# Hybrid decoder block: x loaded by token, plain float32 first products, and turns moved around the rotations and the second norm

## The chip, the cores and the metric

One core of a Trainium2 chip runs the kernel. The metric is the device time of one execution in microseconds (us); three runs are given by their median. The engines are TensorE (PE; its weight loads are PEld), VectorE (DVE), ScalarE (ACT), GpSimd (POOL) and SyncE (SP), whose queue issues nearly all loads.

## The reference

x has 256 tokens of 2048 features, c is one conditioning vector, all float32.

```python
mod = silu(c) @ w_ada + b_ada                       # 2048 -> 6 x 2048
shift1, scale1, gate1, shift2, scale2, gate2 = split(mod, 6)
h = rms_norm(x, norm1_g) * (1 + scale1) + shift1
qa, ka, va, qr, kr, vr, gr, ga_logit, gb_logit = split(h @ w_in, ...)
qa, ka = rms_norm per head                          # 8 heads of 128
ya = softmax(qa ka^T * 128**-0.5 + bias[distance], causal) va @ w_attn_br
qr, kr = rotary(qr), rotary(kr) * 128**-0.5         # 8 heads of 128
yr = (group_norm((qr kr^T * decay) vr) * silu(gr)) @ w_ret_br
x = x + gate1 * ((sigmoid(ga_logit) * ya + sigmoid(gb_logit) * yr) @ w_o)
h2 = rms_norm(x, norm2_g) * (1 + scale2) + shift2
val, gt = split(causal_conv3(h2 @ w_up) + conv_b, 2)     # 2 x 5632
out = x + gate2 * ((silu(gt) * val) @ w_down)
```

## The kernel before, in words

**Products.** A float32 product is made of three products of the type float32r: each operand is split into hi (an ACT cast) and lo (a DVE subtraction, `split`, line 133), and hi hi, lo hi and hi lo are added up in PSUM. Activations are the stationary side (128 features x 128 tokens), weights the moving side (512 columns). Weights come in tiles of 128 x 1024 (512 KB, tag raw, nine buffers, shared with w_ada); such a chunk is 12 products of 512 columns for the two halves of the tokens (t = 0, 1). `row_block` (214) runs one 256 x 512 result through its chunks, with two PSUM banks of eight.

**First norm (231 to 271).** x comes transposed (xT, features on partitions). Squares are summed over the tiles on ACT and DVE, a product with a matrix of ones sums over the partitions, and rstd is 128 x 256. `modulated` (262) loads four halves of w_ada for each 128 features; each half is one DVE product with silu(c), summed into `parts` (`ada`, 170). `norm_tile` (250) then makes scale and shift with single-column operations and multiplies x by rstd (both on POOL from k = 2 on), applies scale and shift on ACT, and splits: h1[k].

**First products (274 to 300).** Six groups of 1024 columns (q, k, rotary q, k, and gr) need h1[0] to h1[10] in the steps k = 0 to 2, 3 to 5 and 6 to 10; in a step each group runs its k's and is added into `acc`. The other five k's follow in `finish_block` (314; 2.5 chunks a block of 512 columns).

**What sets the order.** The code is written once, straight through, and a planner orders each engine's instructions ahead of time by program order, readiness and its own estimate of durations; on the chip every engine then works in that order. `keep_in_program_order` pins an instruction among the pinned ones. The class `Side` (50) mixes in side work: after each chunk `pump` counts down every active generator (`yield 6` sleeps six chunks) and runs those that are due, a little ahead in priority; at most `width` are active, others wait in a queue. A paced generator issues w_ada halves at a rate a chunk (0.75, later 0.46 and 0.38), and `until` forces it.

**Rotations.** After each of the blocks 4 to 7 (499) a generator `rotated(n)` is put at the front of the side queue. It gives POOL, for each t, two multiplications by sin (487), one by cos (489) and one addition (490), sleeps six chunks, and turns the result with 16 transposes (r_t, 339). Blocks 8 to 11 follow (gr, with silu). The attention heads (three active at a time; scores, softmax with scalings on POOL at 452, turn, product with va) share that queue. Retention (514) sleeps three chunks before its turn (rpt, 549).

**Second norm (637 to 663).** Four w_o blocks, each added to x2 with gate1 (642, 643) and squared with a sum on ACT (644); then rstd2 for all tokens, a scaling on DVE (654), transposes (xt, 587), scale and shift on ACT (661) and the split into h2; then 22 blocks of w_up and 8 of w_down.

Of the kernel before, what the change touches and what calls it, by code (L numbers as in the profile page):

```python
# [11 lines left out]
F32 = mybir.dt.float32  # L12
# [17 lines left out]
K2 = STEPS[-1][1]  # L30
ADA_FIRST = 0.75
ADA_RATE = 0.46
ADA_LAST = 0.38
SIDE_AHEAD = 150
FH = FT // 2
# [56 lines left out]
def block_kernel(ctx, tc, a, out):  # L92
# [19 lines left out]
    def bank(name):  # L112
        return psum.tile([P, 512], F32, tag="ps", name=name)
# [6 lines left out]
    xT = cpool.tile([P, KC, S], F32, tag="x", name="xT")  # L120
    for q in range(4):
        nc.sync.dma_start(xT[:, 4 * q:4 * q + 4, :], a["xT"][:, 4 * q:4 * q + 4, :])
    ones = cpool.tile([P, P], F32, name="ones")
    nc.vector.memset(ones, 1.0)
# [5 lines left out]
    mod = cpool.tile([P, NADA], F32, name="mod")  # L130

# [30 lines left out]
    def load_split(src, w, name):  # L162
        raw = wpool.tile([P, 1024], F32, tag="raw", name=f"raw_{name}", bufs=9)
        nc.sync.dma_start(raw[:, :w], src)
        hi = wpool.tile([P, 1024], F32R, tag="hi", name=f"hi_{name}")
# [4 lines left out]
    def ada(jt, pin=False):  # L170

        for h in range(2):
            t = wpool.tile([P, 1024], F32, tag="raw", name=f"ada_{jt}_{h}", bufs=9)
            nc.sync.dma_start(t, a["w_ada"][jt, h])
            ins = nc.vector.scalar_tensor_tensor(t, t, 1.0, crow[:, h * 1024:(h + 1) * 1024],  # L175
                                                 op0=ALU.mult, op1=ALU.mult, accum_out=parts[:, jt, h:h + 1])
            if pin:

                tc.keep_in_program_order(ins)
            yield  # L180
# [7 lines left out]
    def scales_of(eng, j0, n, g_col):  # L188

        m = mod[:, j0:j0 + n]  # L190
        eng.tensor_scalar_add(m, m, 1.0)
        eng.tensor_tensor(m, m, sm[:, g_col:g_col + n], op=ALU.mult)

    def tok(act, part, t):

        return act[part][:, t * P:(t + 1) * P]
# [17 lines left out]
    def row_block(dram, acts, name):  # L214

        ps = [bank(f"{name}_{t}") for t in range(2)]
        n = len(acts)
        for k0 in range(0, n, 2):
# [4 lines left out]
        return ps  # L223

# [6 lines left out]
    sums = []  # L231
    for q in range(8):
        sq = tmp(f"sq1_{q}", (P, 2, S))
        xq = xT[:, 2 * q:2 * q + 2, :]
        if q == 7:
            nc.vector.tensor_tensor(sq, xq, xq, op=ALU.mult)
        else:
            nc.scalar.activation(sq, xq, AF.Square)
        if q > 1:
            nc.vector.tensor_tensor(sq, sq, sums.pop(0), op=ALU.add)  # L240
        sums.append(sq)
    nc.vector.tensor_tensor(sums[1], sums[0], sums[1], op=ALU.add)
    nc.scalar.activation(warm, crow[:, D - 1:], AF.Sqrt, bias=eps, scale=0.0)
    stat = bank("stat1")
    for k in range(2):
        nc.tensor.matmul(stat[:, :S], ones, sums[1][:, k, :], start=(k == 0), stop=(k == 1))
    rstd = cpool.tile([P, S], F32, name="rstd")
    h1 = []

    def norm_tile(k):  # L250
        eng = nc.vector if k < 2 else nc.gpsimd
        mods_of(eng, KC + k, 1)
        mods_of(eng, k, 1)
        scales_of(eng, KC + k, 1, C_G1 + k)
        t = tmp(f"ht_{k}")
        eng.tensor_tensor(t, xT[:, k, :], rstd, op=ALU.mult)
        nc.scalar.activation(t, t, AF.Identity, bias=mod[:, k:k + 1], scale=mod[:, KC + k:KC + k + 1])
        h = unit(f"h1_{k}", F32R)
        split(h[:, 0], h[:, 1], t)
        return h[:, 0], h[:, 1]  # L260

    def modulated():
        for k in range(KC):
            yield from ada(KC + k, pin=(k == 0))
            yield from ada(k, pin=(k == 0))
            h1.append(norm_tile(k))

# [3 lines left out]
    rstd_of(rstd, stat[:, :S], 1.0 / D)  # L271


    acc = [[None, None] for _ in range(2 * NG)]
    for step, (ka, kb) in enumerate(STEPS):
        for g in range(NG):
            banks = [[bank(f"g{step}_{g}_{j}_{t}") for t in range(2)] for j in range(2)]
            for k in range(ka, kb):
                side.until(lambda: len(h1) > k)
                hi, lo = load_split(a["w_g"][k, g], 1024, f"g_{g}_{k}")  # L280
                for part, w in ((0, hi), (1, hi), (0, lo)):
                    for t in range(2):
                        for j in range(2):
                            nc.tensor.matmul(banks[j][t], tok(h1[k], part, t), w[:, j * NB:(j + 1) * NB],  # L284
                                             start=(k == ka and part == 0 and w is hi),
                                             stop=(k == kb - 1 and w is lo))
                side.pump()
            for j in range(2):
                for t in range(2):
                    n = 2 * g + j  # L290
                    if step == 0:
                        acc[n][t] = unit(f"acc_{n}_{t}", shape=(P, NB))
                        nc.scalar.copy(acc[n][t], banks[j][t])
                    elif j == 0:
                        e = tmp(f"ev{step}_{n}_{t}", (P, NB))
                        nc.scalar.copy(e, banks[j][t])
                        nc.gpsimd.tensor_tensor(acc[n][t], acc[n][t], e, op=ALU.add)
                    else:
                        nc.vector.tensor_tensor(acc[n][t], banks[j][t], acc[n][t], op=ALU.add)
# [4 lines left out]
    def rest_of_mod():  # L304
        for jt in range(2 * KC, 6 * KC):
            yield from ada(jt, pin=True)
            if jt % KC == KC - 1:
                j0 = jt + 1 - KC
                mods_of(nc.gpsimd, j0, KC)
                if j0 == 4 * KC:  # L310
                    scales_of(nc.gpsimd, j0, KC, C_G2)
            mods[0] = jt + 1
# [8 lines left out]
    x2 = cpool.tile([P, 2, D], F32, tag="x", name="x2")  # L321
    cosT = cpool.tile([P, 2, P // 2], F32, name="cosT")
    sinT = cpool.tile([P, 2, P], F32, name="sinT")
    for dst, src in ((sm[:, C_CW:], a["small"][:, C_CW:]), (cosT.rearrange("p t d -> p (t d)"), a["cos"]),
                     (sinT.rearrange("p t d -> p (t d)"), a["sin"]), (x2[:, 0], a["x"][0]), (x2[:, 1], a["x"][1])):

        nc.gpsimd.tensor_copy(dst[:, :1], acc[0][0][:, :1])
        nc.sync.dma_start(dst, src)
# [147 lines left out]
    turned = Side(tc, 1)  # L476
    qrT, krT = [None] * 4, [None] * 4

    def rotated(n):
# [11 lines left out]
        yield 6  # L491
# [22 lines left out]
    def retention(h, v):  # L514
# [30 lines left out]
        yield 3  # L545
# [67 lines left out]
    side.drain()  # L613
# [23 lines left out]
    for n in range(4):  # L637
        o = row_block(a["w_o"][n], mT, f"o_{n}")
        for t in range(2):
            xn = x2[:, t, n * NB:(n + 1) * NB]  # L640
            y = tmp(f"og_{n}_{t}", (P, NB))
            nc.vector.tensor_tensor(y, o[t], gate1[n], op=ALU.mult)
            nc.vector.tensor_tensor(xn, xn, y, op=ALU.add)
            nc.scalar.activation(y, xn, AF.Square, accum_out=ssq2[:, 4 * t + n:4 * t + n + 1])
    side.until(lambda: mods[0] >= 5 * KC)
    rstd2 = small("rstd2", 2)
    nc.vector.tensor_reduce(rstd2, ssq2.rearrange("p (t n) -> p t n", n=4), axis=AX.X, op=ALU.add)
    rstd_of(rstd2, rstd2, 1.0 / D)
    h2 = []
    for n in range(4):  # L650
        xs = []
        for t in range(2):
            y = tmp(f"xn_{n}_{t}", (P, NB))
            nc.vector.tensor_scalar_mul(y, x2[:, t, n * NB:(n + 1) * NB], rstd2[:, t:t + 1])  # L654
            xs.append(y)
        for i in range(2):
            pt = pair_bank(f"xt_{n}_{i}", xs, i)
            y = tmp(f"ht2_{n}_{i}", (P, NB))
            for j in range(2):
                k = 4 * n + 2 * i + j  # L660
                nc.scalar.activation(y[:, j * S:(j + 1) * S], pt[:, j * S:(j + 1) * S], AF.Identity,  # L661
                                     bias=mod[:, 3 * KC + k:3 * KC + k + 1], scale=mod[:, 4 * KC + k:4 * KC + k + 1])
            h2 += pair_acts(f"h2_{n}_{i}", y)
# [27 lines left out]
    for half in range(2):  # L691
        gT = []
        for b in range(half * FH // 2, half * FH // 2 + FH // 2):
            ps = row_block(a["w_up"][b], h2, f"up_{b}")
# [116 lines left out]
```

## Time and profile before

| | |
|---|---|
| runs | 1662.76 us median of 3 (1662.49 to 1665.72) |
| profiled execution | 1666.35 us, span 1664.6 us |
| mean granted TensorE clock | 0.987 of full |
| PE busy | 1599.7 us (96%) |
| DVE, ACT, POOL busy | 1149.5, 814.1, 259.5 us |
| moved | 402.95 MB, mean 242 GB/s |

The span is what the profiler sees from the first to the last instruction; the execution's own time is 1.75 us more. In the rows below L136 is line 136 of the kernel; `a <- b` after an engine's wait names what it waited for.

### The profile page before, as it was taken

What the parts mean: (1) busy time and instruction counts of PE and PEld (TensorE: products, weight loads), DVE (VectorE), ACT (ScalarE), POOL (GpSimd) and SP (SyncE); (2) the same over time, 40 slices, a digit from 0 to 9 for tenths busy, and PEclk for the clock granted to TensorE, in tenths of its full rate; (3) what the DMA queues carried; (4) which work ended last, traced back from release to release, by engine and by line L of the source; (5) the groups of instructions that cost most, each with busy time, mean ns of one, the idle gap of its engine ahead of it and who ended that gap; (6) DMA issues with size and microseconds to landing.
All of it is one profiled execution on the core that took longest, in us unless ns stands there. A gap on an engine that the chain in (4) does not pass through costs nothing.

```text
span 1664.6 us, 19951 instructions
## 1 busy us (share of the span) xinstructions
PE 1599.7 (96%) x7144; PEld 1316.1 (79%) x7144; DVE 1149.5 (69%) x1459; ACT 814.1 (49%) x1054; POOL 259.5 (16%) x241
## 2 busy tenths in 40 slices
PE   3998999989999999999998999999999999999998
PEld 1886788867888788888886888888888888888887
DVE  7799897786767766777777577886544555565554
ACT  4653455545545444444444555555433455555432
POOL 3166652285100000000000000000100100000000
PEclk9999999988999999999999999999999999999999
DMA  9998898766766788888887588777666665666661
GB/s 361 325 315 298 314 342 265 246 204 207 270 225 218 258 283 279 277 278 260 293 315 244 163 266 261 259 247 225 212 197 193 190 183 184 190 182 187 200 206 59
DMA packets 114347, 402.95 MB, mean 242 GB/s; under 512 B 12788, under 2 KB 15428, under 8 KB 113992
## 3 DMA queue, kind: packets, MB, share of 16 engines
q1 hardware_dynamic: 112952, 399.51, 73.2%
q10 hardware_dynamic: 1296, 2.17, 0.3%
q8 instruction: 56, 0.92, 0.2%
q14 instruction: 43, 0.35, 0.1%
HBM read 399.51 MB, written 2.13 MB: 241 GB/s over the span
## 4 chain that ended last, share of the span: by engine, by line
PE 66%; DVE 1%; ACT 0%; issue 0%; ACTq 0%
PE up L201 29%; PE dn L201 14%; PE yr L201 5%; PE gb L201 5%; PE o L201 5%; PE ga L201 4%; PE ya L201 1%; PE ut L587 1%; PE xt L587 0%; PE mt L587 0%; DVE lo_up L136 0%; ACT ht L661 0%; DVE xn L654 0%; DVE dg L714 0%; DVE dg L710 0%
## 5 line engine op out<-in xcount | busy, mean ns | idle before, releaser
L136 DVE TENSOR_TENSOR lo_up<-raw_up,hi_up 128x1024 fp32r<-128x1024 f32 x176 | 215.6, 1225 | 170.5 <-ACT hi_up L135 125.1
L135 ACT CAST hi_up<-raw_up 128x1024 fp32r<-128x1024 f32 x176 | 185.5, 1054 | 198.6 <-PE up L201 163.4
L201 PE MATMUL up<-hi_up,h_h 128*128 128x512 f32 x704 | 277.2, 394 | 0.0
L201 PE MATMUL up<-hi_up,h_l 128*128 128x512 f32 x704 | 275.2, 391 | 0.0
L175 DVE SCALAR_TENSOR_TENSOR ada<-ada,crow 128x1024 f32<-128x1024 f32 x192 | 250.0, 1305 | 0.0
L201 PE MATMUL up<-lo_up,h_h 128*128 128x512 f32 x704 | 197.1, 392 | 0.0
L136 DVE TENSOR_TENSOR lo_dn<-raw_dn,hi_dn 128x1024 fp32r<-128x1024 f32 x88 | 107.8, 1225 | 111.4 <-ACT hi_dn L135 107.8
L284 PE MATMUL g<-hi_g,h 128*128 128x512 f32 x528 | 135.6, 399 | 25.3 <-ACT h L135 20.6
L135 ACT CAST hi_dn<-raw_dn 128x1024 fp32r<-128x1024 f32 x88 | 92.8, 1054 | 134.6 <-PE dn L201 117.9
L201 PEld LDWEIGHTS up<-hi_up,h_l 128*128 128x128 f32 x704 | 132.8, 189 | 27.1
L201 PEld LDWEIGHTS up<-lo_up,h_h 128*128 128x128 f32 x704 | 132.4, 188 | 27.2
L201 PEld LDWEIGHTS up<-hi_up,h_h 128*128 128x128 f32 x704 | 132.8, 189 | 26.3
L284 PEld LDWEIGHTS g<-hi_g,h 128*128 128x128 f32 x528 | 100.5, 192 | 51.0 <-ACT h L135 23.0
L201 PE MATMUL dn<-hi_dn,gT_h 128*128 128x512 f32 x352 | 137.2, 390 | 0.0
L201 PE MATMUL dn<-hi_dn,gT_l 128*128 128x512 f32 x352 | 137.0, 389 | 0.0
L684 POOL TENSOR_TENSOR cv<-cv,cv 128x512 f32<-128x512 f32 x22 | 34.3, 1560 | 513.9 <-ACT cv L683 418.6
L185 POOL TENSOR_TENSOR mod<-parts 128x1 f32<-128x1 f32 (+1 forms) x32 | 22.5, 704 | 524.1 <-DVE ada L175 515.3
L136 DVE TENSOR_TENSOR lo_g<-raw_g,hi_g 128x1024 fp32r<-128x1024 f32 x66 | 86.7, 1326 | 17.1 <-ACT hi_g L135 17.1
L201 PE MATMUL dn<-lo_dn,gT_h 128*128 128x512 f32 x352 | 95.6, 389 | 0.0
L135 ACT CAST hi_g<-raw_g 128x1024 fp32r<-128x1024 f32 x66 | 67.4, 1054 | 20.1 <-PE g L284 13.5
L201 PEld LDWEIGHTS dn<-lo_dn,gT_h 128*128 128x128 f32 x352 | 66.1, 188 | 13.7
L201 PEld LDWEIGHTS dn<-hi_dn,gT_h 128*128 128x128 f32 x352 | 66.1, 188 | 13.6
(212 smaller groups left out, 2869.8 us busy)
## 6 DMA issues: line engine op xcount, KB each, us to landing
ada<-in_w_ada SPq DMA_DIRECT2D x192, 512.0 KB, 4.7
raw_up<-in_w_up SPq DMA_DIRECT2D x176, 512.0 KB, 3.9
raw_dn<-in_w_down SPq DMA_DIRECT2D x88, 512.0 KB, 3.7
raw_g<-in_w_g SPq DMA_DIRECT2D x66, 512.0 KB, 5.2
raw_vr<-in_w_vr SPq DMA_DIRECT2D x32, 512.0 KB, 4.8
raw_ga<-in_w_col SPq DMA_DIRECT2D x32, 512.0 KB, 4.4
raw_yr<-in_w_ret_br SPq DMA_DIRECT2D x32, 512.0 KB, 4.5
raw_gb<-in_w_col SPq DMA_DIRECT2D x32, 512.0 KB, 4.4
```

Of the source, the lines that this page charges most:

```text
L135: nc.scalar.copy(hi, src)
L136: nc.vector.tensor_tensor(lo, src, hi.bitcast(F32), op=ALU.subtract)
L175: ins = nc.vector.scalar_tensor_tensor(t, t, 1.0, crow[:, h * 1024:(h + 1) * 1024], op0=ALU.mult, op1=ALU.mult, accum_out=parts[:, jt, h:h ...
L185: eng.tensor_tensor(m, parts[:, j0:j0 + n, 0], parts[:, j0:j0 + n, 1], op=ALU.add)
L201: nc.tensor.matmul(ps[t], tok(acts[k0 + k], part, t), w[:, k * NB:(k + 1) * NB], start=first, stop=last)
L284: nc.tensor.matmul(banks[j][t], tok(h1[k], part, t), w[:, j * NB:(j + 1) * NB], start=(k == ka and part == 0 and w is hi), stop=(k == kb - ...
L587: nc.tensor.transpose(pt[:, (2 * j + t) * P:(2 * j + t + 1) * P], us[t][:, s], ident)
L684: nc.gpsimd.tensor_tensor(cvs[0], cvs[0], cvs[1], op=ALU.mult)
```

## The change

x is loaded once, by token (x2, tokens on partitions); the later load of x goes. Its squares are summed along the rows (ACT for t = 0, DVE for t = 1), rstd is one number a token, and `turn_x` scales 512 features on ACT, turns them on PE and copies them out; two quarters at the start, two after h1[5] and h1[9]. Modulation arithmetic of `norm_tile` is on DVE, pinned, as are all w_ada products. For k below PLAIN = 2 h and w_in go into PE as they are, in float32, without splits. In step 0 groups 0 and 1 run together, k by k, with all eight banks. `rotated` runs at once, and only its turn goes to the side queue, behind block n + 4. Retention sleeps five chunks. The drain ahead of w_o goes. In the last w_o block the last four chunks, and in the first w_up block the first four, do one half of the tokens ahead of the other (`skewed`), and the second norm is made half by half and quarter by quarter in the order of `quads`.

```diff
+PLAIN = 2
+SKEW = 4
...
-    xT = cpool.tile([P, KC, S], F32, tag="x", name="xT")
...
+    x2 = cpool.tile([P, 2, D], F32, tag="x", name="x2")
+    for t in range(2):
+        for q in range(2):
+            nc.sync.dma_start(x2[:, t, q * 1024:(q + 1) * 1024], a["x"][t, :, q * 1024:(q + 1) * 1024])
...
+    def skewed(ps, dram, acts, name, chunks, n, before=None):
+        ws = []
+        for c in chunks:
+            raw = wpool.tile([P, 1024], F32, tag="raw", name=f"raw_{name}_{c}", bufs=9)
+            nc.sync.dma_start(raw, chunk(dram, 2 * c * NB, 2 * NB))
+            for k in range(2):
+                hi, lo = (unit(f"{name}_{c}_{k}_{w}", F32R, (P, NB)) for w in "hl")
+                split(hi, lo, raw[:, k * NB:(k + 1) * NB])
+                ws.append((2 * c + k, hi, lo))
+        for t in range(2):
+            for k, hi, lo in ws:
+                if before is not None and k % 2 == 0:
+                    before(t, k // 2)
+                for part, w in ((0, hi), (1, hi), (0, lo)):
+                    nc.tensor.matmul(ps[t], tok(acts[k], part, t), w, start=(k == 0 and part == 0 and w is hi),
+                                     stop=(k == n - 1 and w is lo))
...
+            yield t
...
     def norm_tile(k):
...
+        m = mod6[:, 0:2, k]
+        pin = tc.keep_in_program_order
+        pin(nc.vector.tensor_tensor(m, parts6[:, 0:2, k, 0], parts6[:, 0:2, k, 1], op=ALU.add))
+        pin(nc.vector.tensor_tensor(m, m, bada6[:, 0:2, k], op=ALU.add))
+        scale = mod6[:, 1, k:k + 1]
+        pin(nc.vector.tensor_tensor(scale, scale, sm[:, C_G1 + k:C_G1 + k + 1], op=ALU.mult))
+        t = plain[:, k] if k < PLAIN else tmp(f"ht_{k}")
...
+    def g_chunk(banks, g, k, first, last):
+        side.until(lambda: len(h1) > k)
+        if k < PLAIN:
+            raw = load(a["w_g"][k, g], 1024, f"g_{g}_{k}")
+            for t in range(2):
+                for j in range(2):
+                    nc.tensor.matmul(banks[j][t], plain[:, k, t * P:(t + 1) * P], raw[:, j * NB:(j + 1) * NB],
+                                     start=first, stop=last)
...
+        for gs in ((0, 1), (2,), (3,), (4,), (5,)) if step == 0 else tuple((g,) for g in range(NG)):
...
     for n in range(4, 8):
         finish_block(n)
-        side.queue.insert(0, rotated(n))
+        rotated(n)
...
     for n in range(8, 12):
         for u in finish_block(n):
             nc.scalar.activation(u, u, AF.Silu)
+        side.queue.insert(0, turn_rotated(n - 4))
...
-        yield 3
+        yield 5
...
         side.add(turn_merged(n))
-    side.drain()
...
+    o = row_block(a["w_o"][3], mT, "o_3", kn=KC - 2 * SKEW)
+    for t in skewed(o, a["w_o"][3], mT, "o_3", range(KC // 2 - SKEW, KC // 2), KC):
+        residual(3, t, o[t])
...
+    quads = [(0, 0), (0, 1), (1, 0), (1, 1), (0, 2), (1, 2), (0, 3), (1, 3)]
+    def turn_h2(t, q):
+        xs = tmp(f"xn_{q}_{t}", (P, NB))
+        nc.vector.tensor_scalar_mul(xs, x2[:, t, q * NB:(q + 1) * NB], rstd2[:, t:t + 1])
+        pt = bank(f"xt_{q}_{t}")
+        for j in range(4):
+            nc.tensor.transpose(pt[:, j * P:(j + 1) * P], xs[:, j * P:(j + 1) * P], ident)
+        y = tmp(f"ht2_{q}_{t}", (P, NB))
+        for j in range(4):
+            k = 4 * q + j
+            nc.scalar.activation(y[:, j * P:(j + 1) * P], pt[:, j * P:(j + 1) * P], AF.Identity,
+                                 bias=mod[:, 3 * KC + k:3 * KC + k + 1], scale=mod[:, 4 * KC + k:4 * KC + k + 1])
+        hl = [unit(f"h2_{q}_{t}_{w}", F32R, (P, NB)) for w in "hl"]
+        split(hl[0], hl[1], y)
...
+        for _ in skewed(ps, dram, h2, "up_0", range(SKEW), KC,
+                        before=lambda t, c: turn_until(2 + c if t == 0 else 4 + c + 1)):
+            pass
```

## Rows read from the trace of the kernel before

**Rows 1.** The profile's page, busy time by engine: us (share of span) xinstructions:

```profile
PE 1599.7 (96%) x7144; PEld 1316.1 (79%) x7144; DVE 1149.5 (69%) x1459; ACT 814.1 (49%) x1054; POOL 259.5 (16%) x241
```

**Rows 2.** TensorE's waits, whole span: us in total, times, longest us:

```profile
PE r_t L339 <- POOL acc L490: 9.0, 2, 7.3
...
PE xt L587 <- DVE xn L654: 7.8, 3, 5.5
...
PE rpt L549 <- ACT yn L544: 4.1, 1, 4.1
...
PE mt L587 <- DVE m L611: 0.8, 1, 0.8
```

**Rows 3.** Windows of TensorE: length, busy (xrecords), granted clock, DMA share, GB/s:

```profile
0.00:31.29 31.29, 5.85 (x13) 1.00 0.94 349
...
31.29:46.08 14.79, 11.38 (x28) 0.88 1.00 371
...
145.87:159.78 13.91, 8.35 (x30) 0.88 0.87 289
...
171.60:232.08 60.48, 57.12 (x245) 1.00 0.92 330
...
363.07:379.03 15.96, 8.69 (x40) 0.68 0.41 127
...
390.63:401.29 10.66, 7.95 (x28) 0.68 0.63 204
...
544.98:555.41 10.43, 6.28 (x21) 0.84 0.75 259
...
904.54:925.00 20.46, 12.66 (x52) 0.67 0.23 77
```

**Rows 4.** The chain of waits, two pieces: start, length, what, xcount:

```profile
584.27 21.76 PE ga L201 x96
...
948.44 0.66 PE ut L587 x6
```

**Rows 5.** Timeline of TensorE, 530 to 532: start, length, operation, tile, shapes, xrecords:

```profile
530.30 0.59 PE L529 MATMUL py<-vr_u,st 128*128 128x256 f32 x2
...
530.73 0.59 PE L530 MATMUL py<-vr_u,st 128*128 128x256 f32 x2
```

**Rows 6.** Windows: PE, PEld, DVE, ACT, POOL busy, then as rows 3:

```profile
10.00:25.00 15.00, 2.07 (x4) 1.17 (x4) 14.90 (x23) 5.03 (x7) 5.70 (x4) 1.00 1.03 412
...
0.00:235.00 235.00, 197.22 (x817) 157.15 (x818) 202.07 (x264) 118.31 (x168) 125.45 (x133) 0.99 0.91 323
```

**Rows 7.** Groups by shape, DVE and ACT: busy us, mean ns | idle:

```profile
L175 DVE SCALAR_TENSOR_TENSOR ada<-ada,crow 128x1024 f32<-128x1024 f32 x192 | 250.0, 1305 | 0.0
...
L136 DVE TENSOR_TENSOR lo_g<-raw_g,hi_g 128x1024 fp32r<-128x1024 f32 x66 | 86.7, 1326 | 17.1 <-ACT hi_g L135 17.1
...
L448 ACT ACTIVATE lg<-lg,mx 128x128 f32<-128x128 f32 x8 | 3.2, 402 | 4.5 <-DVE mx L447 4.5
...
L135 ACT CAST h_h<-ht 128x512 fp32r<-128x512 f32 x8 | 4.8, 630 | 0.0
```

**Rows 8.** Timeline of POOL, around the rotations:

```profile
232.27 1.29 POOL L297 TENSOR_TENSOR acc<-acc,ev 128x512 f32<-128x512 f32 x1 [0.42 <-ACT ev L296]
...
315.21 1.74 POOL L452 TENSOR_SCALAR lg<-lg,rsum 128x128 f32<-128x128 f32 x2 [2.80 <-PE fp L201]
...
317.52 6.52 POOL L452 TENSOR_SCALAR lg<-lg,rsum 128x128 f32<-128x128 f32 x4 [0.56 <-DVE rsum L450]
...
341.19 15.23 POOL L487 TENSOR_TENSOR sw<-acc,sinT 128x256 f32<-128x256 f32 x12 [17.15 <-issue]
...
368.20 9.39 POOL L490 TENSOR_TENSOR acc<-acc,sw 128x512 f32<-128x512 f32 x6
```

**Rows 9.** Timeline of DVE at the second norm:

```profile
904.48 1.28 DVE L642 TENSOR_TENSOR og<-o,gate 128x512 f32<-128x512 f32 x2
...
909.62 1.67 DVE L654 TENSOR_SCALAR xn<-x,rstd 128x512 f32<-128x512 f32 x4
```

More of the change, by code (lines that the diff above doesn't have):

```diff
@@ L228, in rstd_of @@
         nc.vector.reciprocal(dst, dst)
[L231 to L242, printed above, removed]
+    ssq0 = small("ssq0", 8)
@@ L245, in block_kernel @@
-    for k in range(2):
-        nc.tensor.matmul(stat[:, :S], ones, sums[1][:, k, :], start=(k == 0), stop=(k == 1))
-    rstd = cpool.tile([P, S], F32, name="rstd")
     h1 = []
-    def norm_tile(k):
[L251 to L257, printed above, removed]
+    turned = []
@@ L270, in block_kernel @@
         next(side.paced)
[L271 to L287, printed above, removed]
+    rstd = small("rstd", 2)
@@ L288, in block_kernel, with turn_x @@
+    nc.vector.tensor_reduce(rstd, ssq0.rearrange("p (t n) -> p t n", n=4), axis=AX.X, op=ALU.add)
+    rstd_of(rstd, rstd, 1.0 / D)
+    def turn_x(q):
+        xs = []
+        for t in range(2):
+            xs.append(tmp(f"xn1_{q}_{t}", (P, NB)))
+            nc.scalar.activation(xs[t], x2[:, t, q * NB:(q + 1) * NB], AF.Copy, scale=rstd[:, t:t + 1])
+        for i in range(2):
+            pt = bank(f"xn_t{q}_{i}")
             for j in range(2):
                 for t in range(2):
-                    n = 2 * g + j
@@ L291, in block_kernel @@
[L291 to L299, printed above, removed]
+                    s = slice((2 * i + j) * P, (2 * i + j + 1) * P)
@@ new lines, in turn_x @@
+                    nc.tensor.transpose(pt[:, (2 * j + t) * P:(2 * j + t + 1) * P], xs[t][:, s], ident)
+            turned.append(unit(f"xnT_{q}_{i}", shape=(P, NB)))
+            nc.scalar.copy(turned[-1], pt)
+    for q in range(2):
+        turn_x(q)
+    acc = [[None, None] for _ in range(2 * NG)]
+    def g_chunk(banks, g, k, first, last):
+        side.until(lambda: len(h1) > k)
+        if k < PLAIN:
+            raw = load(a["w_g"][k, g], 1024, f"g_{g}_{k}")
+            for t in range(2):
+                for j in range(2):
+                    nc.tensor.matmul(banks[j][t], plain[:, k, t * P:(t + 1) * P], raw[:, j * NB:(j + 1) * NB],
+                                     start=first, stop=last)
+        else:
+            hi, lo = load_split(a["w_g"][k, g], 1024, f"g_{g}_{k}")
+            for part, w in ((0, hi), (1, hi), (0, lo)):
+                for t in range(2):
+                    for j in range(2):
+                        nc.tensor.matmul(banks[j][t], tok(h1[k], part, t), w[:, j * NB:(j + 1) * NB],
+                                         start=(first and part == 0 and w is hi), stop=(last and w is lo))
+        side.pump()
@@ new lines, in g_out @@
+    def g_out(step, g, banks):
+        for j in range(2):
+            for t in range(2):
+                n = 2 * g + j
+                if step == 0:
+                    acc[n][t] = unit(f"acc_{n}_{t}", shape=(P, NB))
+                    nc.scalar.copy(acc[n][t], banks[j][t])
+                elif j == 0:
+                    e = tmp(f"ev{step}_{n}_{t}", (P, NB))
+                    nc.scalar.copy(e, banks[j][t])
+                    nc.gpsimd.tensor_tensor(acc[n][t], acc[n][t], e, op=ALU.add)
+                else:
+                    nc.vector.tensor_tensor(acc[n][t], banks[j][t], acc[n][t], op=ALU.add)
@@ L305, in rest_of_mod @@
         for jt in range(2 * KC, 6 * KC):
-            yield from ada(jt, pin=True)
+            yield from ada(jt)
             if jt % KC == KC - 1:
@@ L648, in block_kernel @@
[L648 to L663, printed above, removed]
+            residual(n, t, o[t])
@@ new lines, in turn_h2 @@
+    def turn_h2(t, q):
[11 more added lines that the diff above has]
+        split(hl[0], hl[1], y)
+        for j in range(4):
+            for part in range(2):
+                h2[4 * q + j][part][t] = hl[part][:, j * P:(j + 1) * P]
@@ L665, in block_kernel, with turn_until, first_up @@
+    def turn_until(n):
+        while quads and 8 - len(quads) < n:
+            turn_h2(*quads.pop(0))
+    def first_up():
+        dram = a["w_up"][0]
+        ps = [bank(f"up_0_{t}") for t in range(2)]
+        for _ in skewed(ps, dram, h2, "up_0", range(SKEW), KC,
+                        before=lambda t, c: turn_until(2 + c if t == 0 else 4 + c + 1)):
+            pass
+        return row_block(dram, h2, "up_0", ps=ps, k1=2 * SKEW, before=lambda k0: turn_until(8))
     side.rate = ADA_LAST
```

97 lines of the change are left out of this document (61 added, 36 removed).

## The prediction

> **What bounds the kernel now.** I read the page's busy shares first, then TensorE's waits, then the clock and the instruction count in the stretches around those waits. TensorE (PE below) is busy for 96% of the span [rows 1], and in the chain of waits 96 products of 512 columns take 21.76 us, six transposes 0.66 us: 0.2267 and 0.11 us each [rows 4]. So the kernel is worth its PE work plus what PE loses, and a loss is both an idle wait and the stretch at a lower granted clock behind it. PE's list of waits is short [rows 2], and the windows price each place [rows 3]: length less (instructions times those two rates; a window's count includes up to two records that only reach into it).
> - First products (tile g): PE starts on them at 31.29. To 46.08 it gets 28 products (6.35 us of work) into 14.79 us: 8.4 lost. From 145.87 to 159.78, again 28 products in 13.91: 7.6 lost. The stage is 792 products, 179.5 us, and the last window of it ends at 232.08, so some 5 more are lost in small waits.
> - Turned rotations (r_t): 363.07 to 379.03 holds 24 transposes and 14 products, 5.8 us of work in 15.96: 10.2 lost. 390.63 to 401.29 loses 6.0 by the same count (15 products, 12 transposes). Together 16.2; the clock column says 0.68, so part of it ran at 1.2 instead of 2.4 GHz.
> - Turned retention (rpt): 10.43 us with 4.4 of work, 6.0 lost.
> - Second norm (xt): 904.54 to 925.00 holds 32 transposes and 18 products, 7.6 us in 20.46: 12.9 lost.
> - Last merged turn (mt): 0.8 idle [rows 2].
> The change touches all five places.
>
> **First products.** Removed: xT and its sums, the product with ones, POOL's multiply and modulation arithmetic ahead of each h tile, the second load of x, and for k = 0 and 1 both splits (12 ACT casts, 12 DVE subtractions). Added: eight squares with sums (four on ACT, four on DVE), 8 scalings and 8 evictions on ACT, 32 transposes (16 before the first product, where PE idles; 16 later, 16 x 0.11 = 1.8 us on the path), three small DVE operations a tile.
> Start: the first product needs x (4 tiles of 0.524 MB) and four w_ada halves. To 31.29 it moves 349 GB/s, or 10.9 MB [rows 3], of which 6.2 in 10 to 25, at 412 [rows 6]; that leaves some 2.4 MB for the first 10 us, so the eighth tile (4.2 MB) lands near 14. DVE then has a 1.3 us product per half [rows 7], four in series after its last squares near 11.3: about 16.5, and I allow 2 us for three small operations and one ACT pass: 18.5. A plain product needs no split, so PE starts there, 12.8 us sooner. The bounds are 16 (DVE keeps up with the DMA) and 31 (nothing gained); I take 18.5 because DVE is the longer of two chains that are both visible. Tiles 14 and 20, which close h1[1] and h1[2], land near 22 and 31, before PE has done the four plain chunks, so two groups at once keep PE fed.
> Work: a float32 product of 256 columns takes two records and 0.43 us [rows 5], so 512 columns take 0.86. A plain chunk is four of them, 3.44 us, against 12 x 0.2267 = 2.72: 12 chunks cost 8.6 more. The start runs at 1.2 GHz for a while, as from 31.29 to 46.08; unbroken work should lose 3.
> Sum: 18.5 + 3 + 54 x 2.72 + 12 x 3.44 + 1.8 = 211.5. Two feeders stand close behind. DVE is busy 202 of the first 235 us [rows 6]; without 12 subtractions of 1.33 it has about 187 to do between 10 and the end, with idle time forced in the plain chunks, where it may run only a few tiles ahead. 66 chunks, 64 halves and x are 70.25 MB, 170 us at 412 GB/s, 217 at the mean 323 [rows 6]. I add 5.5 us of small waits: end at 217, **15 us gained**. Bounds: 212 and 224. The x reload that falls away came when the stage was over; it is worth nothing.
>
> **Rotations.** `rotated` loses its place in the side queue: POOL gets it as soon as a block is done, and only the transposes wait, until after the four silu blocks. Today POOL idles from 324.0 to 341.19 and then needs 36.5 us for three blocks, 12.2 each; six softmax scalings take 8.3 [rows 8]. In the new order the rotations start near 324, but heads 3 to 5 no longer wait behind them, and their scalings and bias copies (about 11) go in between: 324 + 49 + 11 = 384 for the last block. The four turns enter the queue at its front, so the last block, 7, is turned first, when heads 3 to 5 leave their slots. Today's first turn is 17 pump units behind the start of block 4 and stands at 363.07; the new one is 21 units behind, four chunks of 2.72 later at most: near 372 on today's clock. PE's order is fixed in advance, and today PE stands at the first turn until POOL is done (7.3 idle [rows 2]), so the planner counted on a faster POOL. PE would stand again, up to 384 - 372 = 12 us, at these turns or at the heads' own, with a slow stretch behind it; the nearest row is today's pair, 9.0 idle and the rest slow: **15 lost instead of 16, 1 gained**. Bounds: nothing lost (+16) and 24 lost (-8).
> What decides is POOL's pace. Its 128x512 addition takes 1.29 us beside little else and 9.39/6 = 1.57 in the rotations [rows 8]. The Trainium skill, SBUF — State Buffer, section "SBUF: two separate sides", states that VectorE operations with two SBUF inputs and GpSimd operations exclude each other on a shared port pair for a whole instruction, so that one blocks. The trace agrees in direction (1.57 against 1.29), and by that rule the new rotations, which lie beside the same subtractions, keep today's pace and the stall stays. At 1.29 throughout (60 x 1.29/1.57 = 49) POOL would be done near 373 and the stall would be gone, which makes the sum 1618 instead of 1632; that is rival A.
>
> **Retention.** Two more pumps (5.4 us of products) before the turn, against 4.1 idle: **5 gained** of 6. If the planner uses the room for something else, 0. More pumps a head lengthen the side queue; 48 later chunks hide it.
>
> **Merged turn.** No drain; the mt turn comes behind the first w_o chunk: **0.8**. Unpumped w_ada halves are then forced ahead of the last w_o block, two or three of 1.3 us on DVE, hidden by its slack.
>
> **Second norm.** In the last four w_o chunks one half of the tokens ends 24 products (5.4 us) early. From its last product to its scaled x DVE and ACT today need 904.48 to 909.62 for both halves with a subtraction in between [rows 9]; one half needs about 3.3, so it is ready before the products end. Then transposes, four ACT passes and a cast. A 128x128 ACT pass costs 0.40, the cast 0.63 [rows 7]: 2.24 a quarter-half, 17.9 for eight, plus squares and weight casts, against 25 us of PE work in the first up block. So ACT, not PE, paces the start: I give it 4 lost of today's 12.9, **8.9 gained**. Bounds: 2 and 8 lost. The 16 extra split instructions of half size (SKEW chunks) ride on the same engines and are in that number.
>
> **Sum.** 15 + 1 + 5 + 0.8 + 8.9 = 30.7. The profiled execution took 1666.35 us, 3.6 above the median of 1662.76; from it the result is 1635.6, and on the scale of the medians **1632**.
>
> **Rivals.**
> A. POOL keeps up and the rotations' stall goes: 1632 - 14 = 1618. For it: POOL is free 17 us sooner. Against: it starts 17 us sooner but has 11 us more to do, and the last block is asked for first.
> B. The first stage is fed no better than today (323 GB/s, subtractions of 1.33): it ends at 224, 8 gained instead of 15: 1639. For it: DVE 202 of 235. Against: POOL's modulation work, which runs beside those subtractions, is gone.
> C. Slower. All w_ada products are pinned in order on DVE, which works in order: one that waits for its load holds the subtractions and additions queued behind it, and PE starves. DVE has about 16 us of room in the stage (10 to 217 less 187, less some idle that is forced); past 0.25 us of wait a half (64 halves) the end moves one for one, and past 0.75 us the whole 31 us are gone. At 1 us it is 64 - 16 - 31 = 17 later than now: 1680. Against: no idle time stands before any of today's 192, of which 128 are pinned [rows 7].
> D. The new order does not do what it says: the planner puts the turns and the early half where they were, and only moved waits remain: within 3 us of 1662.8.
>
> **How the numbers follow.** Forecast 0.52, A 0.25, B 0.13, C 0.06, D 0.04. The forecast's own range is 1620 to 1645; A reaches down to 1609 if the first stage also ends at 212; B up to 1648. Leaving out C, D and the ends, 1609 to 1648. A measurement of this kernel tells 0.2% (3.3 us) from no change. Faster is forecast, A and B: 0.90; same is D: 0.04; slower is C: 0.06.
>
> **What would show it.** Right: the first plain product between 16 and 22 us; the last g product near 217; no fifteen-us gap before 30; rows like today's 904.54 window with about 4 us lost; PE waits of xt under 3. A wait of PE on POOL acc or lg of several us between 340 and 390 confirms the rotation step; none is rival A. DVE idle before ada, over 16 us in the first 235, is rival C. The forecast fails if the first stage ends after 226 or PE gets a new wait above 5 us outside these places.

## The result, and the profile after

The changed kernel takes 1646.99 us (median of 4 runs, 1646.25 to 1648.13) against 1663.09 us (4 runs) for the one before on the same chip: ratio 0.9896, 95% interval 0.9879 to 0.9913. That is 16.1 us faster by medians and 18.2 by the two profiled executions (1666.35 and 1648.13). The forecast was 1632, its range 1609 to 1648: the sign was right, but little more than half of the 30.7 that were forecast came. The time is near the slow end of the whole range and outside the 1620 to 1645 that the prediction gave the forecast itself.

The page's busy line after answers to [rows 1]: TensorE (PE) does the same work, POOL a third less.

```profile
PE 1600.7 (97%) x7124; PEld 1305.6 (79%) x7124; DVE 1132.1 (69%) x1491; ACT 820.9 (50%) x1090; POOL 177.9 (11%) x142
```

PE's waits after answer to [rows 2] (us in total, times, longest):

```profile
PE xn_t L314 <- ACT xn L308: 15.3, 2, 8.8
PE xt L732 <- DVE xn L729: 8.0, 1, 8.0
PE fp L203 <- DVE lo_fp L140: 6.9, 2, 6.1
```

The waits on r_t, rpt and mt are gone. Three of 6 to 9 us stand there instead: one on xn_t in the first stage (the other part of its 15.3, 6.5, lies before the first product, where PE is idle anyway), one on lo_fp, and xt as before. To see what each part gave, take the view of one tile, which has the first and the last start of its products. Before:

```profile
L201 PE MATMUL fp<-hi_fp,h x240: 387/389/776, 232.1 to 379.3; 128*128 128x512 f32 x120
L201 PE MATMUL ga<-hi_ga,h x256: 387/389/628, 503.1 to 637.8; 128*128 128x512 f32 x128
L201 PE MATMUL o<-hi_o,mT_h x128: 387/389/476, 816.7 to 903.6; 128*128 128x512 f32 x128
L201 PE MATMUL up<-hi_up,h_h x704: 387/389/775, 918.5 to 1538.5; 128*128 128x512 f32 x176
```

After:

```profile
L203 PE MATMUL fp<-hi_fp,h x240: 387/389/792, 222.5 to 371.4; 128*128 128x512 f32 x120
L203 PE MATMUL ga<-hi_ga,h x256: 387/389/580, 494.0 to 618.9; 128*128 128x512 f32 x128
L203 PE MATMUL o<-hi_o,mT_h x112: 389/389/476, 796.5 to 872.4; 128*128 128x512 f32 x112
L203 PE MATMUL up<-hi_up,h_h x688: 387/389/477, 911.7 to 1519.3; 128*128 128x512 f32 x172
```

| stretch (first to last start) | before | after | gained |
|---|---|---|---|
| start to first fp product (first products) | 232.1 | 222.5 | 9.6 |
| first fp to last ga (rotations, retention) | 405.7 | 396.4 | 9.3 |
| last ga to first o (merged turn) | 178.9 | 177.6 | 1.3 |
| first o to last up product (second norm) | 721.8 | 722.8 | -1.0 |

The four sum to 19.2. The spans differ by 19.0 (1664.6 and 1645.6), and the time of an execution outside its span grew by 0.8, which leaves the 18.2.

**First products.** PE's timeline, lines with a wait in brackets:

```profile
18.91 14.00 PE L330 MATMUL g<-raw_g,h_plain 128*128 128x512 f32 x32 [1.17 <-ACT h_plain L282]
...
145.61 0.69 PE L314 MATMUL xn_t<-ident,xn 128*128 128x128 f32 x2 [8.82 <-ACT xn L308]
```

The first product comes at 18.91, as forecast (18.5). Then one stall stands alone, 136.8 to 145.6, and the window over it has PE busy for 6.17 of 15 us at a granted clock of 0.69, DVE for all 15, POOL for none:

```profile
135.00:150.00 15.00, 6.17 (x23) 4.83 (x22) 15.00 (x25) 5.62 (x8) 0.00 (x0) 0.69 0.92 319
```

It stands where [rows 3] has the stall at 145.87, some 9 us earlier. The transposes of the last quarter of x wait for ACT's scaling, and ACT's queue shows why that was late: it stood behind tile 9's pass (ht), which waited for DVE's w_ada sums.

```profile
144.34 0.60 ACT L282 ACTIVATE ht<-xnT,mod 128x256 f32<-128x256 f32 x1 [2.66 <-DVE mod L280]
144.85 1.32 ACT L308 ACTIVATE xn<-x,rstd 128x512 f32<-128x512 f32 x2
```

**Rotations.** POOL is done with them at 362.1 and none of their turns waits. But DVE's timeline shows a new stop, and PE's 6.10 us wait at 355.77 is for the lo_fp behind it:

```profile
343.12 2.32 DVE L184 SCALAR_TENSOR_TENSOR ada<-ada,crow 128x1024 f32<-128x1024 f32 x1
...
345.45 1.14 DVE L140 TENSOR_TENSOR lo_fp<-raw_fp,hi_fp 128x512 fp32r<-128x512 f32 x1
351.07 0.74 DVE L509 SCALAR_TENSOR_TENSOR lg<-sc,ssq,bias 128x128 f32<-128x128 f32 x2 [4.49 <-POOL acc L553]
...
353.45 2.27 DVE L140 TENSOR_TENSOR lo_fp<-raw_fp,hi_fp 128x1024 fp32r<-128x1024 f32 x1
```

The scores (lg) of the later heads wait for POOL's rotation, and the splits of fp stand behind them in DVE's order.

**Second norm.** PE stops at 884.84 and turns the first scaled quarter at 892.86, 8.02 us later. The first half of the tokens was done 24 products, 5.4 us, before the stop, at 879.4. What DVE did from there:

```profile
877.16 4.90 DVE L140 TENSOR_TENSOR up_l<-raw_up,up_h 128x512 fp32r<-128x512 f32 x8
881.98 0.68 DVE L707 TENSOR_TENSOR og<-o,gate 128x512 f32<-128x512 f32 x1
883.50 1.23 DVE L140 TENSOR_TENSOR lo_up<-raw_up,hi_up 128x1024 fp32r<-128x1024 f32 x1 [0.84 <-ACT hi_up L139]
884.64 0.69 DVE L708 TENSOR_TENSOR x<-x,og 128x512 f32<-128x512 f32 x1
885.24 1.22 DVE L140 TENSOR_TENSOR lo_up<-raw_up,hi_up 128x1024 fp32r<-128x1024 f32 x1
886.38 0.68 DVE L707 TENSOR_TENSOR og<-o,gate 128x512 f32<-128x512 f32 x1
886.98 1.22 DVE L140 TENSOR_TENSOR lo_up<-raw_up,hi_up 128x1024 fp32r<-128x1024 f32 x1
888.11 1.22 DVE L184 SCALAR_TENSOR_TENSOR ada<-ada,crow 128x1024 f32<-128x1024 f32 x1
...
889.25 0.15 DVE L721 TENSOR_REDUCE rstd<-ssq 128x1 f32<-128x4 f32 x1
...
891.06 0.16 DVE L253 RECIPROCAL rstd<-rstd 128x1 f32<-128x1 f32 x1
...
892.33 0.48 DVE L729 TENSOR_SCALAR xn<-x,rstd 128x512 f32<-128x512 f32 x1
```

Between each two steps of the chain (og, x, rstd, xn) stands a split or a w_ada product of later work: 12.9 us from 879.4 to 892.33, for steps that need about 3 (2.9 in e9 below).

### The profile page after: what moved, and what is told of

Its sections match the earlier page's. It is cut to its first block, busy times and chain, and to the rows that moved or that the text cites. A ratio compares the mean times of both kernels' runs of the same rounds, so it can differ in the third digit from the quotient of the medians.

```text
span 1645.6 us, 19843 instructions
## 1 busy us (share of the span) xinstructions
PE 1600.7 (97%) x7124; PEld 1305.6 (79%) x7124; DVE 1132.1 (69%) x1491; ACT 820.9 (50%) x1090; POOL 177.9 (11%) x142
## 4 chain that ended last, share of the span: by engine, by line
PE 91%; DVE 3%; POOL 2%; DMA 2%; issue 1%; ACT 1%; SPq 0%; DVEq 0%; ACTq 0%; POOLq 0%
PE up L203 29%; PE dn L203 14%; PE g L337 9%; PE yr L203 5%; PE ga L203 5%; PE gb L203 5%; PE vr L203 5%; PE o L203 4%; PE va L203 3%; PE ya L203 3%; PE fp L203 2%; PE g L330 2%; DVE ada L184 1%; PE ut L653 1%; POOL sw L550 1%
## 5 line engine op out<-in xcount | busy, mean ns | idle before, releaser
L139 ACT CAST hi_up<-raw_up 128x1024 fp32r<-128x1024 f32 x172 | 181.0, 1052 | 187.1 <-PE up L203 157.3
L203 PE MATMUL up<-hi_up,h_h 128*128 128x512 f32 x688 | 269.8, 392 | 0.0
L203 PE MATMUL up<-hi_up,h_l 128*128 128x512 f32 x688 | 268.0, 390 | 0.0
L184 DVE SCALAR_TENSOR_TENSOR ada<-ada,crow 128x1024 f32<-128x1024 f32 x192 | 245.9, 1286 | 1.9 <-DMA ada<-in_w_ada 1.8
L203 PE MATMUL up<-lo_up,h_h 128*128 128x512 f32 x688 | 193.1, 392 | 0.0
L337 PE MATMUL g<-hi_g,h 128*128 128x512 f32 x432 | 110.8, 398 | 1.7 <-ACT hi_g L139 1.7
L337 PEld LDWEIGHTS g<-hi_g,h 128*128 128x128 f32 x432 | 81.8, 190 | 21.0 <-ACT hi_g L139 2.5
L139 ACT CAST hi_g<-raw_g 128x1024 fp32r<-128x1024 f32 x54 | 56.9, 1055 | 59.4 <-PE g L337 43.3
L140 DVE TENSOR_TENSOR lo_g<-raw_g,hi_g 128x1024 fp32r<-128x1024 f32 x54 | 71.6, 1333 | 17.6 <-ACT hi_g L139 17.6
L203 PEld LDWEIGHTS dn<-hi_dn,gT_l 128*128 128x128 f32 x352 | 66.1, 188 | 13.7
L203 PEld LDWEIGHTS dn<-hi_dn,gT_h 128*128 128x128 f32 x352 | 66.1, 188 | 13.6
```

What stands on the lines that cost most here:

```text
L139: nc.scalar.copy(hi, src)
L140: nc.vector.tensor_tensor(lo, src, hi.bitcast(F32), op=ALU.subtract)
L184: tc.keep_in_program_order(nc.vector.scalar_tensor_tensor(t, t, 1.0, crow[:, h * 1024:(h + 1) * 1024], op0=ALU.mult, op1=ALU.mult, accum_o ...
L203: nc.tensor.matmul(ps[t], tok(acts[k0 + k], part, t), w[:, k * NB:(k + 1) * NB], start=first, stop=last)
```

## The experiments

All compute the whole function. Times are medians; the kernel before took 1663.5 to 1665.9 in these comparisons and 1663.09 in the first, so a difference of 2 or 3 us between runs of different comparisons is not firm by medians alone. The stages come from one profiled execution of each run; the end of the first stage, the same in eight of them, lies between 221.5 and 222.5, so a stage tells about 1 us.

**e1: the front alone.** The changed kernel with the four later parts as before.

> The changed front (x by token, plain products for k = 0 and 1) with the old rotations in the side queue, the old drain, the old 3 pumps before the rpt turn and the old second norm. Theory (by the stage ends in the two traces: last g product 9.5 us earlier, everything from there to the second norm another 9.5 to 10, the second norm nothing): about 1654, 1651 to 1656. Rival 1: the stall at the rotations is tied to the start, so the front alone loses its gain at the rotations: 1660 or more. Rival 2: the front makes all of the gain, and the later parts only moved waits: 1647.

Measured 1655.09 (1654.29 to 1655.69), ratio 0.9936 [0.9924, 0.9949]. The theory held: front and later parts add up. From first fp to last ga it takes 404.7 us, as before within 1:

```profile
L203 PE MATMUL fp<-hi_fp,h x240: 387/389/775, 221.9 to 369.7; 128*128 128x512 f32 x120
L203 PE MATMUL ga<-hi_ga,h x256: 387/389/628, 491.9 to 626.6; 128*128 128x512 f32 x128
```

**e2: the second norm as before.**

> The changed kernel with the second norm of before (w_o blocks in one order for both halves, one rstd for both halves, first up block not skewed). Theory: the half that was meant to run ahead got nothing, since DVE's fixed order puts up splits and w_ada products between the steps of its chain; the norm loses about 13 us either way: 1645 to 1649. Rival: the early half did its 9 us and they were lost at another place: 1655 or more.

Measured 1647.85 (1647.26 to 1648.56); first o to last up product 723.5 us against 722.8. The theory held: the running ahead of one half is worth nothing as it stands.

**e3: a buffer of its own for the rotations.**

```diff
-            sw = tmp(f"sw_{n}_{t}", (P, 4, 2, P // 2))
+            sw = tpool.tile([P, 4, 2, P // 2], F32, tag="sw", name=f"sw_{n}_{t}", bufs=1)
```

> The changed kernel with the rotations' scratch tile in one buffer of its own, outside the ring of six that the attention scores use (one unit buffer less, 45, to make room). Theory: PE's wait of 6.1 us for DVE near 350, and the slow stretch behind it, come from scores that wait for a ring buffer that a queued rotation holds, with the splits of fp behind them on DVE; the wait goes: 6 to 9 us faster than the changed kernel, 1638 to 1641. Rival: it is POOL's order and pace (bias copies and score scalings behind the rotations): within 2 us of the changed kernel, 1645 to 1649, with the wait still there.

Measured 1644.99 (1644.17 to 1645.95), 2.0 below the changed kernel and at the rival's end; first fp to last ga takes 393.9 us for 396.4. The wait on lo_fp went, as the theory has it, and came back at the scores' turn, on POOL, as the rival has it:

```profile
PE pt L521 <- POOL lg L516: 7.5, 2, 5.2
```

The ring tied the waits to DVE; behind it stands POOL, whose window is full (columns: busy us of PE, PEld, DVE, ACT, POOL):

```profile
340.00:350.00 10.00, 10.00 (x46) 8.29 (x45) 8.88 (x17) 9.64 (x17) 9.84 (x9) 1.00 0.68 212
350.00:360.00 10.00, 4.24 (x19) 3.00 (x17) 7.25 (x9) 5.49 (x8) 10.00 (x9) 0.90 0.85 273
```

**e8: the score scalings from POOL to ACT**, on e3.

```diff
-            nc.gpsimd.tensor_scalar_mul(lg[:, s], lg[:, s], rs[:, t:t + 1])
+            nc.scalar.activation(lg[:, s], lg[:, s], AF.Copy, scale=rs[:, t:t + 1])
```

> The kernel of e3_sw_own with the scaling of the scores by their sums moved from POOL to ACT. Theory: in e3 PE waits 5.2 and 2.4 us for those scalings because POOL is full from 330 to 360 and they stand between rotations; without them the waits and the slow clock go: 6 to 9 us faster than e3, 1636 to 1639. Rival: ACT's own queue (weight casts, Exp and Silu passes) is as late as POOL was: 1642 to 1647.

Measured 1636.68 (1635.59 to 1637.59), ratio 0.9831 [0.9816, 0.9846], 8.3 us below e3. The fp products now run from 221.9 to 360.0, 138 us against 149 in the changed kernel, and PE's waits from 222 to 362 sum to 0.5 us. From first fp to last ga it takes 386.6. POOL works on rotations to 362.9, as late as in the changed kernel, and nobody waits for it. The scalings on ACT with the old ring of six were not tried, nor were scalings ahead of the rotations in POOL's order. One other thing changes in this place: at the heads' Exp and the blocks' Silu (L512, L568) ACT loads a table (ACT_TABLE_LOAD) nine times in the changed kernel, 1.28 us each, and three times in the one before, since the two now alternate. That is not what e8 gained by: e3 and e8 have five each.

**e6: the rotations back in the side queue**, on the changed kernel.

> The changed kernel with the rotations back in the side queue, 6 pumps ahead of their turn, as before; all else as changed. Theory: the new order only put the wait for POOL from the turned rotations (r_t) into the splits of fp, worth nothing either way: 1645 to 1649, with r_t waits of about 9 us in place of the 6.1 us wait on lo_fp. Rival: the rotations gained as much as the late stages show, some 8 us: 1653 to 1657, and the retention's two pumps are then worth nothing.

Measured 1648.21 (1647.24 to 1648.87): the theory held. The waits are those of [rows 2] again,

```profile
PE r_t L403 <- POOL acc L553: 9.2, 3, 7.3
```

and from first fp to last ga it takes 397.1 us against 396.4:

```profile
L203 PE MATMUL fp<-hi_fp,h x240: 387/389/775, 222.1 to 369.9; 128*128 128x512 f32 x120
L203 PE MATMUL ga<-hi_ga,h x256: 387/389/578, 488.5 to 619.2; 128*128 128x512 f32 x128
```

The new order is worth 0.7, which is no more than stages differ by themselves. The same stretch of e1, 404.7, has only the retention's two pumps less: they are worth 7.6.

**e4: the later turns of x earlier.**

```diff
-            if k in (5, 9):
-                turn_x(k // 4 + 1)
+            if k in (3, 7):
+                turn_x(k // 4 + 2)
```

> The changed kernel with the third and fourth turn of x behind tiles 3 and 7 instead of 5 and 9, so that the transposes stand earlier in PE's order. Theory: DVE is full from 100 to 150 us, tile 9 of h1 is late by itself, and PE waits for that tile where it waited for the transposes: the first stage ends where it did, within 3 us: 1644 to 1649. Rival: the 8.8 us wait on xn_t and the slow clock behind it come from the place of the transposes alone: 9 to 12 us faster, 1635 to 1638.

Measured 1643.43 (1643.20 to 1644.09), just under the theory's range: the stage ends at 218.8 instead of 222.5, 3.7 earlier, where the theory allowed 3. The place of the transposes cost that; the rest of the stall stayed, now as waits on hi_g (3.9 us longest).

**e7: a faster w_ada pace in the whole stage**, `ADA_FIRST = 1.0` for 0.75.

> The changed kernel with w_ada paced at 1.0 instead of 0.75 halves a chunk in the first stage. Theory: the stall near 137 to 150 is a burst: at 0.75 about 35 halves are done when the third step asks for tiles 6 to 10 (44 halves) within five chunks, and DVE (full there, idle a fifth of the time before) cannot do nine halves and five splits in 13.6 us; at 1.0 there are 42 and the stall and its slow stretch go: 8 to 12 us faster than the changed kernel, 1635 to 1639. Rival 1: the stage is bound by DVE's or the loads' total, and what is saved there comes back before its end: 1644 to 1649. Rival 2: the faster pace starves the splits earlier in the stage: over 1650.

Measured 1651.39 (1650.45 to 1652.50), slower: rival 2. The stall did go (PE busy 14.13 of 15 from 135 to 150), so the burst of tiles made it. But PE now waits for lo_g all along:

```profile
PE g L337 <- DVE lo_g L140: 10.1, 10, 2.3
```

DVE is busy for 24 of each 25 us from 85 to 210, so what it does for w_ada there it takes from the splits. The pace can only be raised where DVE has room.

**e10: no plain products**, `PLAIN = 0`.

> The changed kernel with no plain products: tiles 0 and 1 of h1 are split like the others. Theory: the plain chunks cost 12 x 0.72 = 8.6 us of PE work, but what they save DVE (12 subtractions of 1.33) is what this stage is short of: without them DVE and the loads bound it and PE waits for lo_g instead; the stage ends at 221 to 226: 1646 to 1651. Rival: PE bounds the stage, and 5 to 8 us are gained: 1639 to 1642.

Measured 1648.58 (1648.11 to 1650.32). The first product comes at 20.62, the stage ends at 225.0, 2.5 later than with the plain ones, though PE has 8.6 us less to do: the theory held. The casts and subtractions of two tiles are dearer here than PE's float32 products (the start alone is 1.7 later).

**e5: DVE's and ACT's order at the second norm, first try.** The splits of up chunks 4 to 7 are held behind the norm (pinned in program order on both engines), `side.rate = 0.0` ahead of the last w_o block, `ADA_RATE = 0.5`.

> The changed kernel with DVE's and ACT's order mended around the second norm: the later up splits (chunks 4 to 7) are held behind the chain of the norm in the order of both engines, no w_ada product is paced in beside it, and the 5 halves that were forced ahead of the last w_o block are spread before it (rate 0.5 for 0.46). Theory: the early half's chain took 13 us instead of 3.3 only because other work stood between its steps; the first scaled x comes near 883 instead of 892, PE's 8 us wait on xt goes and some 4 of 13.5 us stay lost: 1636 to 1641. Rival 1: ACT paces the start (about 2.1 us for the passes and the cast of each of eight quarters), half the loss stays: 1642 to 1645. Rival 2: it is not the order: 1646 to 1649.

Measured 1649.31 (1646.58 to 1650.78), just above rival 2's range, though not by its cause. The profiled execution is the fastest of the six. DVE's timeline:

```profile
880.43 0.16 DVE L255 RECIPROCAL rstd<-rstd 128x1 f32<-128x1 f32 x1 [0.36 <-ACT rstd L254]
883.14 0.69 DVE L709 TENSOR_TENSOR og<-o,gate 128x512 f32<-128x512 f32 x1 [2.55 <-PE o L246]
883.75 0.48 DVE L732 TENSOR_SCALAR xn<-x,rstd 128x512 f32<-128x512 f32 x1
```

The first half's rstd is there at 880.6, but the second half's gating, which waits for PE, stands ahead of the scaling. The first up product came 94.3 us behind the first o product instead of 99.8, and the lead was lost again where PE waited 3.3 us for a pinned hi_up: to the last up product it takes 723.0, as in the changed kernel (722.8).

**e9: the chain whole**, on e8: the scaled quarters of a half are asked for right behind its rstd, the second half's gating is pinned behind them, and the later up splits come one by one. `side.rate = 0.0` and `ADA_RATE = 0.5` are as in e5.

```diff
-        residual(3, t, o[t])
+        residual(3, t, o[t], tc.keep_in_program_order)
         ...
         rstd_of(r, r, 1.0 / D)
+        for q in range(2):
+            scaled(t, q)
```

> The kernel of e8_scale_act with the norm's chain whole on DVE: the first half's two scaled quarters are asked for before the second half's gating, which is held behind them; no w_ada product beside it; the splits of up chunks 4 to 7 come one by one behind the quarters that are due before them, not behind all of them as in e5. Theory: in e5 the first half's rstd was there at 880.6, 3.6 us behind its last product, but the scaled x stood behind the second half's gating until 883.75, and the later splits, held too far back, cost 3 to 4 us again; with both mended PE loses 4 to 5 us of 13.5: 8 to 10 us faster than e8, 1627 to 1629. Rival: ACT, with 2.1 us a quarter-half, paces the first up block whatever DVE's order: 1632 to 1637.

Measured 1634.23 (1633.18 to 1634.91): 2.5 below e8, the rival's range. First o to last up product takes 717.7, 4.3 less than in e8; first fp to last ga takes 388.0, 1.4 more, and the w_ada rate is what changed there. DVE's chain is 2.9 us now (og 870.25, xn 873.18), PE turns both quarters at 875.50, and ACT does this (timeline):

```profile
877.15 0.63 ACT L711 ACTIVATE og<-x 128x512 f32<-128x512 f32 x1 [4.20 <-DVE x L710]
...
878.10 0.29 ACT L254 ACTIVATE rstd<-rstd,eps 128x1 f32<-128x1 f32 x1 [0.22 <-DVE rstd L730]
878.30 2.89 ACT L748 ACTIVATE ht<-xt,mod 128x128 f32<-128x128 f32 x8
881.04 1.17 ACT L139 CAST h_h<-ht 128x512 fp32r<-128x512 f32 x2
```

It is ACT's order, not its load: it idles 4.20 us for the second half's square, and two quarters' passes come before either cast. PE waits 5.21.

**e11: all together**: e9 with e4's turns and

```diff
+        if step == 1:
+            side.rate = 0.75
```

behind `ADA_FIRST = 1.0`.

> All that helped together: e9 with the third and fourth turn of x behind tiles 3 and 7 (e4) and w_ada at 1.0 halves a chunk in the first of the three steps alone, 0.75 after it, so that the burst of tiles 6 to 10 is smaller by some 4 halves without the starved splits of e7 between 85 and 135. Theory: the gains lie in separate stages and add up: e9 less 3.6 (e4) and less up to 3 for the pace: 5 to 7 us faster than e9, 1620 to 1624 if e9 is at its 1627 to 1629. Rival: DVE's total bounds the first stage, and neither moves its end by more than 3.6: within 4 us of e9.

Measured 1628.06 (1626.80 to 1630.62), 6.2 below e9, as the theory has the difference. The first stage ends at 213.6, 8.1 earlier than in e9. If e4's 3.7 holds here too, the pace has the other 4.4, more than expected; no run has it alone.

**e12: ACT's order**, on e11: the first quarter's passes and cast are asked for before the second half's square, which is pinned behind them; the first up splits are asked for there too, and the second half's gating is no longer pinned.

> The kernel of e11_all with ACT's order mended too: the second half's square is held behind the first quarter's passes and cast, where in e9 and e11 ACT stood idle until the second half's square and root were done and then ran two quarters' passes before their casts. Theory: PE's 5.2 us wait on the first h_h becomes about 2, the rest of the start as in e11: 2 to 4 us faster than e11, 1624 to 1626. Rival: the second half is then late by as much, or ACT paces the block anyway: 1627 to 1629.

Measured 1625.75 (1623.87 to 1628.81), ratio 0.9770 [0.9755, 0.9784]. By medians 2.3 below e11, with ranges that overlap; the stages show it: first o to last up 715.8 against 717.3, PE's wait 1.87 for 5.2.

```profile
L205 PE MATMUL o<-hi_o,mT_h x112: 387/389/476, 780.1 to 856.0; 128*128 128x512 f32 x112
L205 PE MATMUL up<-hi_up,h_h x688: 389/389/495, 886.8 to 1495.9; 128*128 128x512 f32 x172
```

ACT's timeline:

```profile
868.97 1.51 ACT L746 ACTIVATE ht<-xt,mod 128x128 f32<-128x128 f32 x4 [3.25 <-PE xt L742]
870.51 0.62 ACT L139 CAST h_h<-ht 128x512 fp32r<-128x512 f32 x1
871.03 0.62 ACT L717 ACTIVATE og<-x 128x512 f32<-128x512 f32 x1
```

This version beats both kernels.

## Why the prediction was right or wrong

| term | forecast | measured | from |
|---|---|---|---|
| first products | 15 | 9.6 | stage ends, before and after |
| rotations | 1 | 0.7 | e6 against after |
| retention | 5 | 7.6 | e1 against e6 |
| merged turn | 0.8 | 1.3 | last ga to first o |
| second norm | 8.9 | -1.0 | first o to last up; e2 |
| sum | 30.7 | 18.2 | the terms |

That the terms sum to the 18.2 of the profiled executions is chance: first fp to last ga has 1.0 more than its two terms (405.7 to 404.7 in e1, which changes nothing there), and the time outside the span takes 0.8 back.

- **First products.** The start (18.5, measured 18.91), the price of the plain chunks (3.44; four took 14.00) and the work were right. The step that failed is "I add 5.5 us of small waits", with the 3 for the start: they were not small, nor at the start. Of these 8.5 the stage made 13.6 (222.5 less 18.9 and 190.0 of work), and the window 135 to 150, with 15 products and 8 transposes, 4.3 us of work, has 10.7 of them in one place. I had read that stall in [rows 3] and let it go with the other small ones. Its cause is in the order of the work: the third step asks for tiles 6 to 10 within five chunks, ahead of the pace, and between 124 and 150.3 DVE does ten w_ada products beside the splits (e7 takes the stall away, and e11 leaves one wait of 2.1 without e7's new ones). Rival B's end, 224, was near, and the subtractions did stay at 1.33 us, but that was not the bound: e11 ends at 213.6 with as many loads and subtractions, these at 1.26.
- **Rotations.** The number was right, the place half right. "PE would stand again, up to 384 - 372 = 12 us, at these turns or at the heads' own": it stood at neither, but 6.1 us at the splits of fp, in DVE's order behind the scores that POOL kept waiting. POOL was not done near 384 but at 362; it started at 307, not 324. Rival A's condition came true (no wait at r_t) and its gain did not. e8 shows the 10 us that lay there (386.6 for 396.4); they came with work taken off POOL, and this new order of it gave 0.7.
- **Retention.** The mechanism was right; its term was mis-sized, 7.6 for 5, by more than the 6.0 that the window of [rows 3] showed; what the other 1.6 are, no run shows.
- **Second norm.** The step that failed: "one half needs about 3.3, so it is ready before the products end". The chain does need 2.9 (e9), but I priced it as if DVE were free for it. DVE works in an order fixed in advance, and of the 16 splits of half size that I counted as load eight stood ahead of the chain, with four later whole splits and two w_ada products between its steps. "ACT, not PE, paces the start" fell too, as far as it meant load: ACT is busy for 10.5 of the 19 us from 893 to 912, and in e12 for 19.7 of the 27 from 868 to 895, where PE has 24.4. e12 gains by order. Mended, the part is worth 6.0 against before (721.8 to 715.8): 6.9 of 12.9 stay lost, inside the bounds of 2 and 8. The part as forecast lost 13.9 and lay outside them.
- **Slower (rival C).** The pinned w_ada products did not wait for loads: 1.9 us of idle time in all stand before the 64 of the first stage.
- **The range.** That the time fell into it is in part luck: its slow end was meant for a first stage that ends at 224, and it took up the second norm's loss. Its fast end has no sum: A's 1618 with a first stage that ends at 212 is 1613, not 1609. Of its own signs two speak against it: "a new wait above 5 us outside these places" is there at lo_fp (6.1), and xt, which was to wait under 3, waited 8.0.

## What to carry to other kernels

Work that is made ready early gains nothing if the engines that finish it have fixed orders with other work between the steps: read the order of every engine on the chain, and hold the filling work behind it. Where a wait only changes its place (r_t, lo_fp, pt), look for the engine that is full in all the variants, and take work off that one. A paced side task that is forced at a later point makes a burst there: raise its pace where the engine has room, and only there.

## What the runs showed of the hardware

Some DVE instructions took about twice their time beside POOL. In the rows of the changed kernel above, a w_ada product took 2.32 us at 343.12 and a 128x1024 split 2.27 at 353.45, with POOL busy throughout; in the window 135 to 150, where POOL does nothing, these cost 1.21 and 1.22:

```profile
139.44 1.21 DVE L184 SCALAR_TENSOR_TENSOR ada<-ada,crow 128x1024 f32<-128x1024 f32 x1
...
143.02 1.22 DVE L140 TENSOR_TENSOR lo_g<-raw_g,hi_g 128x1024 fp32r<-128x1024 f32 x1
```

POOL pays as well: its 128x256 bias copy took 0.39 us at 352.79, beside DVE's sums from PSUM, and 1.39 at 358.28, beside a split:

```profile
352.79 0.39 POOL L472 COPY bias<-brev 128x256 f32<-128x256 f32 x1
...
358.28 1.39 POOL L472 COPY bias<-brev 128x256 f32<-128x256 f32 x1
```

Not every DVE instruction is slowed: a split beside two of POOL's cos products kept its usual time, and those two took 3.63 us, where one took 1.26 at 351.58.

```profile
341.99 1.22 DVE L140 TENSOR_TENSOR lo_fp<-raw_fp,hi_fp 128x1024 fp32r<-128x1024 f32 x1
...
340.73 3.63 POOL L552 TENSOR_TENSOR acc<-acc,cosT 128x512 f32<-128x512 f32 x2
```

The prediction took 1.57 against 1.29 from such a mean; one instruction shows steps of a whole instruction. The Trainium skill, SBUF — State Buffer, section "SBUF: two separate sides", says that the shared port pair is locked for a whole instruction; these rows agree. The same section says that ACT never waits at it. The trace of e8 agrees: the eight pairs of scalings that it moved to ACT took 0.79 to 0.81 us, where POOL took 1.50 to 3.53 for a pair. Which share of its 8.3 us comes from the port and which from POOL's shorter queue, no run tells apart.

The float32 products ran at their full price from their first record: 32 records in 14.00 us are 0.4375 each, as in [rows 5], at a granted clock of 1.00, where I had allowed 3 us for a slow start.
